# Query tiles 0 and 1 as a pair in the gates' ring, and projection steps spread over the attention's units

## The chip, the cores and the metric

The kernel runs on one core of a Trainium2 chip. The metric is the time of one execution on the device in microseconds, the median of several runs. Before the change it is 1763.04 us (three runs, 1761.94 to 1768.70).

## What is computed

One layer of a decoder trunk on 2048 rows of 1024 numbers in float32. A condition vector shifts and scales the rows; one wide product with `W_in` makes the queries, keys, values, the input of a pooling branch and four gates; sliding-window attention (16 query heads in 2 key/value groups, window 128, learned bias, one sink per head) and a causal pooling with four window widths run side by side; both are gated, projected, merged, projected again and normalised.

```python
u = x * (1.0 + scale[:, None, :]) + shift[:, None, :]
h = u @ w_in[l]
q, k, v, a_gate, p_in, p_gate, m_a, m_p = jnp.split(h, offsets, axis=-1)
a = sliding_window_sink_attention(q, k, v, sinks[l], bias, mask) * jax.nn.silu(a_gate)
a = a @ w_attn_proj[l]
p = jnp.einsum('bsgc,gcd->bsgd', multiscale_causal_pool(p_in), w_pool_mix[l]).reshape(B, S, POOL_WIDTH)
p = (p * pool_scale[l]) * jax.nn.silu(p_gate)
p = p @ w_pool_proj[l]
y = jax.nn.sigmoid(m_a) * a + jax.nn.sigmoid(m_p) * p
y = (y @ w_out[l]) * (1.0 + gate[:, None, :])
x = layer_norm(DEEPNORM_ALPHA * x + y, ln_gain[l], ln_bias[l])
```

## The kernel before

**Numbers and tiles.** Every float32 operand of a large product is split into a rounded part `hi` and a remainder `lo`, and each product is made of three matmuls, hi·hi, hi·lo and lo·hi (`mm3`, L138). One matmul takes a 128x128 weight block and 512 moving columns. The rows are worked on in two halves `s` = 0, 1 of 1024, each of two column tiles `t` (in the attention `st`) of 512. The output columns of `W_in` come in tiles `m` of 128: query tiles 0 to 7, one tile of keys, one of values, and eight each for the four gates.

**The ring.** A `Quad` (L276) is a pair of weight tiles. Its four output blocks (two weight tiles `mi` by two column tiles `t`) are made with seven block products in place of eight, in the manner of Strassen and Winograd: named by the moving set that each uses, B11, T1, T2, B21, T3, B22 and T4. Each block product is 4 x 3 = 12 matmuls (`product`, L336), so a pair costs 84 matmuls where the plain way costs 4 x 24 = 96. Its weights need sums of blocks (`sum1`, `mid`, `late`, on GpSimd) and three splits of 1024 columns and one of 512 (`pair_split`, `half_split`: hi on ScalarE, lo on VectorE). `ring` (L470) works through groups of two pairs, `front` opens a group (B11, T1), `back` finishes it, and `consume` takes each of the four blocks as it is ready, in the order (0,0), (1,1), (0,1), (1,0) of (`mi`, `t`). Other work hangs on counted positions (`hooks`, `steps`); in the second half the last group is finished pair by pair (`finish_pairs`, L433).

**Order of the halves.** For each half a ring makes keys, values and gates (17 pairs, nine groups, one of which has a single pair; in the first half the key/value pair is the first of the last group), the gates go to DRAM (`gates_d`), `first_q` (L735) makes query tile 0 the plain way, 48 matmuls for both column tiles, and then `attention` (L750) runs.

**The attention.** It has N = 64 units of one query block and two heads, numbered `n`; `j = n // 8` is the query tile that it uses. A unit's TensorE order is: scores of `n` (`score_mms`), transposes of the exponentials of unit n-2 (`turn_mms`), a piece of projection, values of unit n-2 (`value_mms`). Between the transposes and the values, ScalarE rounds the transposed block into `pth` and VectorE subtracts it into `ptl`. The projection pieces make the pooling tiles (`mix`, whose weights were folded with the pooling mix into `wmix_d`) and query tiles 1 to 7: 30 slots (tile, column tile) of 24 matmuls, two units to a slot, so every unit from 0 to 59 has 12 projection matmuls. Afterwards come the first products of the next ring (`fill_one`).

**What follows a slot.** `take_q` (L771) scales a finished query tile into the halves of `qs`: two ScalarE instructions, then two on VectorE. A pooling slot is followed by `pool_sums` (a ScalarE copy and up to four GpSimd additions), `pool_diff` (one on VectorE) and `finish` (GpSimd, then stores). A query tile's weights are loaded by `fetch`, rounded on ScalarE one unit later and subtracted on GpSimd another unit later. Engines work in program order: `pe`, `act`, `dve`, `pool` and `sp` are wrappers that keep it (L46); loads on `nc.sync` may be placed by the scheduler.

Of the kernel before, what the change touches and what calls it, by code (L numbers as in the profile page):

```python
# [19 lines left out]
P = 128  # L20
# [39 lines left out]
def kernel(  # L60
# [59 lines left out]
    ain_d = [set_store(f"ain{s}") for s in range(2)]  # L120
    pin_d = [set_store(f"pin{s}") for s in range(2)]
    gates_d = {n: dp.tile([2, KT, 2, P, CH], F32, name=f"{n}_d") for n in ("ag", "pg", "ma", "mp")}
    y_d = dp.tile([S // P, P, KT, P], F32, name="y_d")

    def cols(t, n):
# [606 lines left out]
    def moving_u():  # L732
        return (sets["B11"], sets["B21"]), (sets["T2"], sets["B22"])

    def first_q(ph, turn=None):  # L735

        raw, hi, lo = ph.spare(), ph.split(), ph.split()
        nc.sync.dma_start(raw, win[TQ])
        nc.scalar.copy(hi, raw)
        low(nc.vector, lo, raw, hi)  # L740
        accs = []
        for us in moving_u():
            acc, part = projection(us)
            part((hi, lo), 0, KT)
            if turn and not accs:
                turn(1)
            accs.append(acc)
        return accs

    def attention(ph, s, q0, nxt):  # L750
        tp = ph.t
        us = moving_u()
# [4 lines left out]
            nc.sync.dma_start(x, src)  # L757
            return x

        def fetch(kind, m):  # L760
            hi, lo = ph.split(), ph.split()
# [108 lines left out]
        slots = []  # L870
        for j in range(KT):
            slots += [("mix", j, 0), ("mix", j, 1)]
            if j + 1 < KT:
                slots += [("q", j + 1, 0), ("q", j + 1, 1)]
# [8 lines left out]
        tiles = {0: fetch(*slots[0][:2])}  # L883
# [36 lines left out]

        for n in range(N + 5):
            j, t, b = n // U, n // NB % 2, n % NB
            if n < N:
                lgs[n] = score_mms(j, n % U, b, qs[j, t])
            pt = None
# [67 lines left out]
            if pt is not None:  # L993
                pvs[n - 2] = value_mms((n - 2) // U, (n - 2) % U, k0, pth, ptl)


            w = n // 4 + 1
            if n % 4 == 0 and 2 * w < len(slots):
                tiles[w] = fetch(*slots[2 * w][:2])
            if w in tiles and tiles[w][0] is not None:  # L1000
                raw, hi, lo = tiles[w]
                if n % 4 == 1:
                    act.copy(by_two(hi), raw)
                if n % 4 == 2:
                    low(pool, by_two(lo), raw, by_two(hi))
            if n % U == 2 and j + 1 < KT:
                bts[j + 1] = bias_tile(j + 1)
            for st in range(2):
                if n % U == 6 + 2 * st - (U if st else 0) and (m := j + 1 - st) < KT and ("q", m, st) in accs:
                    qs[m, st] = take_q(accs.pop(("q", m, st)))  # L1010
            for what in puts:
                put(pool if n >= 64 else sp, *what)
            puts.clear()
# [10 lines left out]
            for st in range(2):  # L1024
                if n % U == 3 + 2 * st and (j, st) in sums:
                    pgs[j, st] = ld("pg", gates_d["pg"][s, j, st])
                if n % U == ((4, 6 + (j + 1 < KT))[st]) and (j, st) in sums:
                    pl = pool_diff(j, sums.pop((j, st)), accs.pop(("mix", j, st)))
                    finish("p", pin_d[s], j, st, pl, pgs.pop((j, st)))
            for st in range(2):  # L1030
                if n % U == 2 + 2 * st and ("mix", j, st) in accs:
                    sums[j, st] = pool_sums(j, st, accs["mix", j, st])
# [84 lines left out]
    def modulate(u, k):  # L1117
        dve.tensor_scalar(u, u, mod[:, 8 + k : 9 + k], mod[:, k : k + 1], ALU.mult, ALU.add)

    def gate_quads(s):  # L1120
        kv, turn = kv_quad(s)
        quads = [kv] if s else []
# [3 lines left out]
        last = quads[15:] if s else [kv, quads[15]]  # L1126
        return [quads[i : i + 2] for i in range(0, 14, 2)] + [quads[14:15], last], turn

    def gate_modulation(ph, m, cb):
        wa = []  # L1130
# [12 lines left out]
    def head(ph):  # L1143
# [90 lines left out]
            minus(xs[i][0], ts[i], xs[i][0])  # L1234
            minus(xs[4 + i][0], xs[4 + i][0], ts[i])

        groups, turn = gate_quads(0)
        grp = groups[0]
        opened = [[bank(), bank(), None, None] for q in grp]

# [71 lines left out]
        return groups, turn, opened, cb, rest  # L1312

    def first_phase(ph, groups, turn, opened, cb, rest):
# [28 lines left out]
        return ring(ph, groups, opened, hooks, [], lambda tick: first_q(ph, turn))  # L1343

    def second_phase(ph, opened, groups, turn):
        hooks = {(0, (8, 10)[i]): [lambda i=i: turn(i)] for i in range(2)}
        for p, name, half in ((0, "T3", 0), (1, "T3", 1), (3, "T4", 0), (5, "T4", 1)):
            hooks.setdefault((0, p), []).append(lambda name=name, half=half: fill_set(name, half, u1_d[name], sp))
        cb = ph.t.tile([P, D], F32, tag="cb", bufs=1, name="cb")

        def gate_rows():
            nc.scalar.dma_start(gate_d.rearrange("k p -> p k"), mod[:, 16:24], allow_slow_non_contiguous=True)
            nc.scalar.dma_start(cb, gate_d.rearrange("k p -> (k p)").partition_broadcast(P))

        hooks[(0, 2)] = [gate_rows]

        def load_wo(x, k):
            for n in range(2):
                sp.dma_start(cols(x, n), wout[k, n])

        halves_of = [(name, half) for name in set_names[:-1] for half in range(2)]
        for i in range(4):
            ks = (i, 4 + i)
            todo = sums_to(
                ph,
                wo_d,
                i,
                lambda x, r, ks=ks: load_wo(x, ks[r]),
                lambda x, r: dve.tensor_tensor(x, x, cb, ALU.mult),
                False,  # L1370
            )
# [6 lines left out]
        return ring(ph, groups, opened, hooks, [], lambda tick: first_q(ph), True)  # L1378

    def pairs(make):  # L1380
        return [[make(m), make(m + 2)] for m in (0, 4)]
# [130 lines left out]
```

## Time and profile before

| what | value |
|---|---|
| median of three runs | 1763.04 us |
| the profiled execution, its own time | 1766.1 us |
| its span, first to last instruction | 1763.9 us |
| VectorE, ScalarE, GpSimd busy in the span | 1206.9, 934.1, 794.2 us |
| first ring of gates, about | 52 to 401 us |
| first attention, about | 418 to 687 us |
| second ring, about | 696 to 1012 us |
| second attention, about | 1018 to 1285 us |
| output projections and norm | to 1764 us |

The stretches are read from the timeline of TensorE by the names of what its matmuls write and read: `lg<-kk,qs` are the attention's scores, `pt<-ident,L` its transposes, `pv<-pth,vv` and `pv<-ptl,vv` its values, `mm<-set,w_set` and `lg<-set,w_set` the products of the rings and of the projections. A duration of a matmul row spans its whole passage; matmuls overlap, so what one costs is the distance from start to start.

### The profile page before, as it was taken

The numbers are of one execution on the slowest core, as the hardware profiler recorded it, in microseconds if no ns is written. First come the engines' busy times: TensorE is split into PE (matmuls) and PEld (weight loads), VectorE is DVE, ScalarE is ACT, GpSimd is POOL, SyncE is SP. The second block draws the span as 40 slices with busy tenths as digits, with TensorE's granted clock in tenths as the row PEclk, the third lists the DMA queues.
The fourth block names the chain that finished last, engine by engine and source line by source line (L and its number), as shares of the span: only waits on it lengthen the run. The fifth ranks groups of instructions, "written<-read, shape, count | busy, mean of one in ns | idle before, by whom it ended". The sixth has DMA issues, their size and how long they took to land. (4 is left out here: it accounts for less than half of the span.)

```text
span 1763.9 us, 24990 instructions
## 1 busy us (share of the span) xinstructions
PE 1702.4 (97%) x8248; PEld 1427.4 (81%) x8248; DVE 1206.9 (68%) x2178; ACT 934.1 (53%) x1973; POOL 794.2 (45%) x618
## 2 busy tenths in 40 slices
PE   6899999999999998999999999999999989999997
PEld 5688888878888887888788888888888867888785
DVE  5977665655777776766655367777867676764777
ACT  4644444545777775544444377777734343423452
POOL 2154444431356567534434125456763562364542
PEclk9999999999999999999999999999999999999998
DMA  9385767844354567787777634544796675789442
GB/s 364 117 289 174 269 208 270 273 145 132 108 174 147 171 217 288 249 288 253 258 264 261 232 96 135 177 159 141 265 349 215 197 256 169 240 302 386 162 143 108
DMA packets 180466, 381.30 MB, mean 216 GB/s; under 512 B 18785, under 2 KB 39281, under 8 KB 180337
## 3 DMA queue, kind: packets, MB, share of 16 engines
q1 hardware_dynamic: 173696, 363.92, 60.5%
q0 software_dynamic: 3552, 11.56, 1.7%
q10 hardware_dynamic: 3088, 4.23, 0.8%
q8 instruction: 65, 1.06, 0.3%
q14 instruction: 65, 0.52, 0.1%
HBM read 244.35 MB, written 138.44 MB: 217 GB/s over the span
## 5 line engine op out<-in xcount | busy, mean ns | idle before, releaser
L56 PE MATMUL mm<-set_B,w_set 128*128 128x512 f32 x3240 | 798.7, 395 | 14.5 <-ACT u L376 6.3
L56 PEld LDWEIGHTS mm<-set_B,w_set 128*128 128x128 f32 x3240 | 603.3, 189 | 142.6 <-DVE w_set L132 10.3
L56 PE MATMUL lg<-set_T,w_set 128*128 128x512 f32 x2088 | 509.1, 394 | 18.4 <-DVE w_set L132 11.0
L56 PEld LDWEIGHTS lg<-set_T,w_set 128*128 128x128 f32 x2088 | 391.4, 189 | 111.0 <-DVE w_set L132 17.9
L132 DVE TENSOR_TENSOR w_set<-W,w_set 128x1024 fp32r<-128x1024 f32 x162 | 227.9, 1407 | 185.8 <-ACT w_set L325 180.8
L325 ACT CAST w_set<-W 128x1024 fp32r<-128x1024 f32 x162 | 169.8, 1049 | 251.6 <-PE mm L56 190.3
L56 PE MATMUL mm<-set_T,w_set 128*128 128x512 f32 x1080 | 265.5, 394 | 0.0
L56 PEld LDWEIGHTS mm<-set_T,w_set 128*128 128x128 f32 x1080 | 200.5, 188 | 41.0
L294 POOL TENSOR_TENSOR W<-W,A 128x512 f32<-128x512 f32 x56 | 82.1, 1466 | 227.6 <-DMA W<-in_win_dram 63.6
L303 POOL TENSOR_TENSOR W<-W 128x512 f32<-128x512 f32 x56 | 80.5, 1438 | 174.5 <-DVE w_set L132 165.2
L56 DVE TENSOR_TENSOR o<-pv,o 64x128 f32<-64x128 f32 x256 | 72.3, 283 | 89.8 <-ACT o L56 86.9
L56 ACT ACTIVATE L<-L,nm 128x257 f32<-128x257 f32 (+1 forms) x256 | 127.1, 498 | 9.3 <-DVE nm L56 3.9
L298 POOL TENSOR_TENSOR W<-W 128x512 f32<-128x512 f32 x56 | 90.5, 1618 | 84.7 <-DVE w_set L132 75.6
L56 DVE CUSTOM_DVE_ANT_0 L<-lg,bt,nsink 128x256 f32<-128x256 f32 (+1 forms) x256 | 111.6, 473 | 5.0 <-PE lg L56 0.8
L299 POOL TENSOR_TENSOR W<-W 128x512 f32<-128x512 f32 x56 | 84.7, 1513 | 37.9 <-DMA W<-in_win_dram 21.9
L56 POOL TENSOR_TENSOR w_set<-W,w_set 128x1024 fp32r<-128x1024 f32 x14 | 33.7, 2404 | 139.6 <-ACT w_set L56 96.9
L56 POOL TENSOR_TENSOR p<-nxt,pg 128x512 f32<-128x512 f32 x32 | 41.7, 1302 | 105.5 <-DVE sm L56 101.8
L56 ACT COPY o<-pv 64x256 f32<-64x256 f32 x128 | 47.3, 370 | 78.0 <-PE pv L56 77.2
L56 DVE TENSOR_TENSOR ptl<-pt,pth 128x512 fp32r<-128x512 f32 (+1 forms) x128 | 85.7, 669 | 1.9 <-ACT pth L56 1.7
L56 PE MATMUL lg<-kk,qs 128*128 128x256 f32 (+1 forms) x512 | 80.5, 279 | 0.0
L56 ACT ACTIVATE L<-L,sm 128x256 f32<-128x256 f32 (+1 forms) x128 | 64.2, 502 | 29.8 <-DVE sm L56 29.8
L56 ACT CAST pth<-pt 128x512 fp32r<-128x512 f32 (+1 forms) x128 | 73.5, 574 | 10.3
(212 smaller groups left out, 2296.3 us busy)
## 6 DMA issues: line engine op xcount, KB each, us to landing
W<-in_win_dram SPq DMA_DIRECT2D x48, 512.0 KB, 5.5
w_set<-wmix_d SPq DMA_DIRECT2D x32, 512.0 KB, 5.4
W<-in_win_dram SPq DMA_DIRECT2D x34, 256.0 KB, 3.7
A<-in_win_dram SPq DMA_DIRECT2D x34, 256.0 KB, 5.1
ag_d<-sig SPq DMA_DIRECT2D x32, 256.0 KB, 3.8
pg_d<-sig SPq DMA_DIRECT2D x32, 256.0 KB, 4.0
ma_d<-sig SPq DMA_DIRECT2D x32, 256.0 KB, 4.0
mp_d<-sig SPq DMA_DIRECT2D x32, 256.0 KB, 4.0
```

What stands on the lines that cost most here:

```text
L56: return lambda *args, **kw: self.tc.keep_in_program_order(op(*args, **kw))
L132: engine.tensor_tensor(dst, src, as32(hi), ALU.subtract)
L294: e.tensor_tensor(self.w[:, 1, :], self.w[:, 2, :], self.a22, ALU.add)
L298: e.tensor_tensor(x[:, 1, :], x[:, 1, :], x[:, 0, :], ALU.subtract)
L299: e.tensor_tensor(x[:, 2, :], x[:, 0, :], x[:, 2, :], ALU.subtract)
L303: e.tensor_tensor(x[:, 3, :], x[:, 3, :], x[:, 1, :], ALU.subtract)
L325: a.copy(by_two(hi), raw)
```

## The change

Three things are altered.

1. `first_q` goes. Query tiles 0 and 1 become the 18th pair of the ring (`q_quad`), in the last group of each half. The two blocks of tile 0 stay in PSUM and are handed to the attention; the two of tile 1 are stored to DRAM (`q_d`), straight from the ring's tile for one and through a ScalarE copy for the other.
2. In the attention, tile 1 is loaded back from `q_d` two units ahead and taken by `take_q` in units 6 and 8. The slots for query tile 1 go: 28 slots remain, in the order mix 0, mix 1, q 2, mix 2, q 3, ... q 7, mix 7.
3. The 28 x 8 = 224 projection steps (three matmuls each) are spread by `upto` over units 0 to 59: unit 0 has 7 steps, now ahead of its scores, each later one 3 or 4. What follows a slot is timed by `done`, the unit in which the slot ends: `take_q` one unit later, `pool_sums` one, the gate's load two, `pool_diff` three or four. The weights of the first slot (mix 0) go into a buffer `W` of the ring in place of two of the split weights' buffers.

```diff
+    q_d = [dp.tile([2, 2, P, CH], F32, name=f"q{s}_d") for s in range(2)]
...
-    def first_q(ph, turn=None):
-
-        raw, hi, lo = ph.spare(), ph.split(), ph.split()
-        nc.sync.dma_start(raw, win[TQ])
-        nc.scalar.copy(hi, raw)
-        low(nc.vector, lo, raw, hi)
...
-            part((hi, lo), 0, KT)
...
+        order = (("mix", 0), ("mix", 1), ("q", 2), ("mix", 2), ("q", 3), ("mix", 3), ("q", 4), ("mix", 4), ("q", 5), ("mix", 5), ("q", 6), ("mix", 6), ("q", 7), ("mix", 7))
+        slots = [(kind, m, st) for kind, m in order for st in range(2)]
...
+        def upto(n):
+            return (0 if n == 0 else min(n + 1, 61)) * KT * len(slots) // 61
+
+        def unit_of(k):
+            return next(n for n in range(60) if upto(n + 1) > k)
+
+        first = [unit_of(KT * i) for i in range(len(slots))]
+        done = {x: unit_of(KT * i + KT - 1) for i, x in enumerate(slots)}
+
+        def project(n):
+            k = upto(n)
+            while k < upto(n + 1):
+                i = k // KT
+                end = min(KT * (i + 1), upto(n + 1))
+                if k == KT * i:
+                    accs[slots[i]], parts[i] = projection(us[slots[i][2]])
+                parts[i](tiles[i // 2][1:], k - KT * i, end - KT * i)
+                k = end
+
+        room = ph.weights().rearrange("p a c -> p (a c)").bitcast(F32R)
+        tiles = {0: fetch(*order[0], [cols2(room, n) for n in range(2)])}
...
+            if n == 0:
+                project(n)
...
-            i = n // 2
-            if i < len(slots):
-                kind, m, st = slots[i]
-                if n % 2 == 0:
-                    accs[kind, m, st], parts[i] = projection(us[st])
-                parts[i](tiles[i // 2][1:], 4 * (n % 2), 4 * (n % 2) + 4)
+            if 0 < n < 60:
+                project(n)
...
+            for w in range(1, len(order)):
+                at = first[2 * w - 2]
+                if n == at:
+                    tiles[w] = fetch(*order[w])
+                if n in (at + 1, at + 2) and tiles[w][0] is not None:
+                    raw, hi, lo = tiles[w]
+                    if n == at + 1:
+                        act.copy(by_two(hi), raw)
+                    else:
+                        low(pool, by_two(lo), raw, by_two(hi))
...
+            for m in range(1, 2):
+                for st in range(2):
+                    at = 8 * m - 2 + 2 * st
+                    if n == at - 2:
+                        raw_q[m, st] = ld("raw_q", q_d[s][m, st])
+                    if n == at:
+                        qs[m, st] = take_q(raw_q.pop((m, st)))
+            for x in [x for x in done if x[0] == "q" and n == done[x] + 1]:
+                qs[x[1:]] = take_q(accs.pop(x))
...
+                if n == at + 3 + (st == 1 and m + 1 < KT):
+                    pl = pool_diff(m, sums.pop((m, st)), accs.pop(x))
...
+    def q_quad(s, m, first):
+
+
+        def consume(ph, mi, t, src):
+            k = m + mi
+            if k == 0:
+                first[t] = src
+                return
+            x = src
+            if (mi, t) != (1, 1):
+                x = ph.c("qk")
+                nc.scalar.copy(x, src)
+            defer(2, lambda: sp.dma_start(q_d[s][k, t], x))
+
+        return Quad((win[TQ + m], win[TQ + m + 1]), consume)
...
+        quads += [q_quad(s, m, q0) for m in (0,)]
+        if s == 0:
+            quads.insert(-1, kv)
+        return [quads[i : i + 2] for i in range(0, len(quads), 2)], turn, q0
```

More of the change, by code (lines that the diff above doesn't have):

```diff
@@ L733, in moving_u @@
         return (sets["B11"], sets["B21"]), (sets["T2"], sets["B22"])
-    def first_q(ph, turn=None):
-        raw, hi, lo = ph.spare(), ph.split(), ph.split()
-        nc.sync.dma_start(raw, win[TQ])
-        nc.scalar.copy(hi, raw)
-        low(nc.vector, lo, raw, hi)
-        accs = []
-        for us in moving_u():
-            acc, part = projection(us)
-            part((hi, lo), 0, KT)
[L745 to L748, printed above, removed]
     def attention(ph, s, q0, nxt):
@@ L758, in ld, with fetch @@
             return x
-        def fetch(kind, m):
-            hi, lo = ph.split(), ph.split()
+        def fetch(kind, m, lent=None):
+            hi, lo = lent or (ph.split(), ph.split())
             if kind == "mix":
@@ L879, in stage @@
             return tp.tile([P, CH], F32, tag=f"{kind}{half}{t}", bufs=1, name=f"{kind}{half}{t}")
+        def upto(n):
[15 more added lines that the diff above has]
+        tiles = {0: fetch(*order[0], [cols2(room, n) for n in range(2)])}
         qs = {(0, t): take_q(q0[t]) for t in range(2)}
         bts = {0: bias_tile(0)}
-        tiles = {0: fetch(*slots[0][:2])}
+        raw_q = {}
         parts, accs, sums = {}, {}, {}
@@ L994, in attention @@
                 pvs[n - 2] = value_mms((n - 2) // U, (n - 2) % U, k0, pth, ptl)
[L997 to L1005, printed above, removed]
+            for w in range(1, len(order)):
[8 more added lines that the diff above has]
+                        low(pool, by_two(lo), raw, by_two(hi))
             if n % U == 2 and j + 1 < KT:
                 bts[j + 1] = bias_tile(j + 1)
-            for st in range(2):
-                if n % U == 6 + 2 * st - (U if st else 0) and (m := j + 1 - st) < KT and ("q", m, st) in accs:
-                    qs[m, st] = take_q(accs.pop(("q", m, st)))
+            for m in range(1, 2):
[7 more added lines that the diff above has]
+                qs[x[1:]] = take_q(accs.pop(x))
             for what in puts:
@@ L1023, in attention @@
                 act.copy(opened[0][4], opened[0][0])
[L1024 to L1032, printed above, removed]
+            for x, at in done.items():
+                kind, m, st = x
+                if kind == "q":
+                    continue
+                if n == at + 2:
+                    pgs[m, st] = ld("pg", gates_d["pg"][s, m, st])
+                if n == at + 3 + (st == 1 and m + 1 < KT):
+                    pl = pool_diff(m, sums.pop((m, st)), accs.pop(x))
+                    finish("p", pin_d[s], m, st, pl, pgs.pop((m, st)))
+            for x, at in done.items():
+                if x[0] == "mix" and n == at + 1:
+                    sums[x[1:]] = pool_sums(*x[1:], accs[x])
             for x in [x for x in outs if n == x[0] * U + x[1] * NB + NB + 2]:
@@ L1235, in rest_sums @@
             minus(xs[4 + i][0], xs[4 + i][0], ts[i])
-        groups, turn = gate_quads(0)
+        groups, turn, q0 = gate_quads(0)
         grp = groups[0]
@@ L1311, in head, with first_phase @@
         ]
-        return groups, turn, opened, cb, rest
-    def first_phase(ph, groups, turn, opened, cb, rest):
+        return groups, turn, q0, opened, cb, rest
+    def first_phase(ph, groups, turn, q0, opened, cb, rest):
         hooks = {}
@@ L1342, in first_phase, with second_phase @@
             at(-1, 3 + half, lambda half=half: build(ph, "T2", half, b12_d))
-        return ring(ph, groups, opened, hooks, [], lambda tick: first_q(ph, turn))
-    def second_phase(ph, opened, groups, turn):
+        ring(ph, groups, opened, hooks, [], lambda tick: turn(1))
+        return q0
+    def second_phase(ph, opened, groups, turn, q0):
         hooks = {(0, (8, 10)[i]): [lambda i=i: turn(i)] for i in range(2)}
@@ L1377, in second_phase @@
             hooks.setdefault((-1, 3 + half), []).append(lambda half=half: fill_set("T2", half, u1_d["B12"]))
-        return ring(ph, groups, opened, hooks, [], lambda tick: first_q(ph), True)
+        ring(ph, groups, opened, hooks, [], None, True)
+        return q0
     def pairs(make):
```

8 lines of the change are left out of this document (1 added, 7 removed).

## The prediction

> **What bounds the kernel now.** I read the page's head and the engines' busy time, then stretches of the span, then the chain of waits for the price of a matmul, then the timeline unit by unit.
>
> ```profile
> span 1763.9 us, 24990 instructions
> PE 1702.4 (97%) x8248; PEld 1427.4 (81%) x8248; DVE 1206.9 (68%) x2178; ACT 934.1 (53%) x1973; POOL 794.2 (45%) x618
> ```
>
> ```profile
> 200.00:380.00 180.00, 177.70 (x831) 147.30 (x830) 106.68 (x106) 78.34 (x119) 83.47 (x63) 1.00 0.71 245
> 430.00:500.00 70.00, 70.00 (x403) 61.42 (x402) 51.81 (x166) 52.28 (x161) 29.79 (x25) 1.00 0.40 125
> 600.00:700.00 100.00, 93.44 (x514) 80.30 (x513) 76.19 (x206) 68.47 (x192) 70.85 (x60) 0.97 0.69 245
> 860.00:1000.00 140.00, 138.37 (x610) 113.92 (x609) 78.45 (x78) 64.18 (x100) 53.05 (x36) 1.00 0.73 258
> 1000.00:1200.00 200.00, 200.00 (x1126) 174.51 (x1125) 133.14 (x422) 143.07 (x418) 81.87 (x63) 1.00 0.47 146
> ```
>
> The columns after the stretch's length are the busy times of TensorE, its weight loads, VectorE, ScalarE and GpSimd, the granted clock, the DMA share and GB/s. In the rings TensorE is busy but for 1 or 2%; in both attentions it never rests. So removed matmuls count in full, as long as nothing takes their place as the thing waited for. The price of one:
>
> ```profile
> 1470.77 2.72 PE mm L56 x12
> 1478.93 10.88 PE mm L56 x48
> ```
>
> 2.72 / 12 = 0.227 us (the 0.39 us of the groups' rows is passage, not pitch).
>
> A full TensorE says nothing of how near its inputs come to being late. That is read from three neighbouring units of the second attention, 8, 9 and 10, whose values end at 1053, 1057 and 1061 us:
>
> ```profile
> 1050.28 3.02 PE L56 MATMUL mm<-set_B,w_set 128*128 128x512 f32 x12
> 1053.25 0.29 PE L56 MATMUL pv<-ptl,vv 128*128 128x256 f32 x1
> 1054.45 3.02 PE L56 MATMUL mm<-set_B,w_set 128*128 128x512 f32 x12
> 1057.43 0.29 PE L56 MATMUL pv<-ptl,vv 128*128 128x256 f32 x1
> 1058.63 3.00 PE L56 MATMUL mm<-set_T,w_set 128*128 128x512 f32 x12
> 1061.58 0.29 PE L56 MATMUL pv<-ptl,vv 128*128 128x256 f32 x1
> ...
> 1051.48 0.69 DVE L56 TENSOR_TENSOR ptl<-pt,pth 128x512 fp32r<-128x512 f32 x1
> 1053.49 1.39 DVE L56 SCALAR_TENSOR_TENSOR qs<-mm,qs 64x512 fp32r<-64x512 f32 x2 [0.86 <-ACT qs L56]
> 1054.89 0.17 DVE L56 RECIPROCAL sm<-sm 128x2 f32<-128x2 f32 x1
> 1056.51 0.68 DVE L56 TENSOR_TENSOR ptl<-pt,pth 128x512 fp32r<-128x512 f32 x1
> 1060.29 0.68 DVE L56 TENSOR_TENSOR ptl<-pt,pth 128x512 fp32r<-128x512 f32 x1
> ...
> 1052.27 1.18 ACT L56 ACTIVATE qs<-mm 64x512 fp32r<-64x512 f32 x2
> 1055.15 0.51 ACT L56 ACTIVATE L<-L,sm 128x256 f32<-128x256 f32 x1 [0.95 <-DVE sm L56]
> 1055.68 0.59 ACT L56 CAST pth<-pt 128x512 fp32r<-128x512 f32 x1
> 1057.40 1.03 ACT L56 CAST w_set<-W 128x1024 fp32r<-128x1024 f32 x1
> ```
>
> The values need `ptl`; the slack is from the end of `ptl` to the start of `pv<-ptl`. Unit 8, with nothing extra before it: 1051.48 + 0.69 = 1052.17 to 1053.25, **1.08 us**. Unit 9, behind a `take_q`: 1057.19 to 1057.43, **0.24 us**. The take holds ScalarE and then, in series, VectorE; the reciprocal comes only at 1054.89, the scaling, `pth` and `ptl` are queued behind it, and TensorE waits for `ptl`. Unit 10, behind the rounding of a query tile's weights (1057.40): 1060.97 to 1061.58, **0.61 us**. With 12 projection matmuls as cover, none of these is late.
>
> **The change part by part.**
>
> *Matmuls.* Per half the ring's pair costs 84 and `first_q`'s 48 go: +36. The attention loses two slots: -48. Net -12, in both halves -24: 24 x 0.227 = **-5.4 us**.
>
> *The ring's other work.* The pair adds two more splits of 1024, one of 512, four GpSimd sums, two evictions. All lie under 84 matmuls (19 us) in stretches where VectorE is busy 78 of 140 us, ScalarE 64 and GpSimd 53; a split costs 1.4 + 1.05 us by the rows below. Nothing for that, and 1 or 2 us if the cover failed. The odd single pair becomes a full group; the ring's late part already shows no wait there.
>
> ```profile
> L132 DVE TENSOR_TENSOR w_set<-W,w_set 128x1024 fp32r<-128x1024 f32 x162 | 227.9, 1407 | 185.8 <-ACT w_set L325 180.8
> L325 ACT CAST w_set<-W 128x1024 fp32r<-128x1024 f32 x162 | 169.8, 1049 | 251.6 <-PE mm L56 190.3
> ```
>
> *DMAs.* The two query tiles' weights are loaded in another shape with the same bytes; each half adds two stores and two loads of 256 KB. On SP's queue the first bias tiles now stand behind the store of `qk`, where they stood behind the last store of a gate; both follow the last product's eviction.
>
> *The attention's opening.* Before, from the end of the last T4 (400.76 + 5.75 less its tail, 406.3) to the first score are 48 matmuls and a transpose; now 21 matmuls. What must fit under them:
>
> ```profile
> 400.76 5.75 PE L56 MATMUL lg<-set_T,w_set 128*128 128x512 f32 x24
> 417.75 0.56 PE L56 MATMUL lg<-kk,qs 128*128 128x128 f32 x4
> 424.62 0.38 PE L56 MATMUL pt<-ident,L 128*128 128x128 f32 x2
> ...
> 407.55 1.03 SPq L56 DMA_DIRECT2D bt<-e_rep  x2
> ...
> 420.60 0.35 DVE L56 CUSTOM_DVE_ANT_0 L<-lg,bt,nsink 128x128 f32<-128x128 f32 x1
> 422.85 0.28 DVE L56 TENSOR_SCALAR L<-L,sm 128x128 f32<-128x128 f32 x1
> ...
> bt<-e_rep SPq DMA_DIRECT2D x2, 256.0 KB, 4.9
> ```
>
> Counted from the end of T4: the value turn and 21 matmuls end near 5.2 us. The four takes need 4 x 0.6 on ScalarE and 4 x 0.7 on VectorE, near 5.1. The bias tile is issued at 1.3 and lands 4.9 later, 6.2. From the first VectorE step to the scaled block are 423.13 - 420.60 = 2.5 us: 8.7. The first transposes stand behind two scores and 12 more matmuls, near 9.3. It fits by half a microsecond: 0, at most 3 us a half if the bias tile comes late.
>
> *The spread.* 224 steps over 61 don't come out even. Unit 0 has 21 matmuls; of units 1 to 59, 40 have 12 and 19 have 9 (units 2, 5, 8 and so on to 56). A unit with 9 covers 3 x 0.227 = 0.68 us less. The plain slack of 1.08 bears it. The slack of 0.24 behind a take doesn't: 0.44 us of wait, whether the short unit is the one behind the take or the one that holds it, since the take starts when ScalarE is through with its own unit's exponentials, which hang on the scores, not on the projection. `done` puts the takes in units 6, 8, 10, 13, 19, 21, 28, 30, 37, 39, 45, 47, 54 and 56. By the short units next to them:
>
> - 10, 19, 28, 47, 56: 0.44 each, 2.20.
> - 8 and 37 hold a `pool_diff` too, on VectorE between the take and the reciprocal; before, takes and these never met. It takes 0.60 (666.33 to 666.93 below): 1.04 each, 2.08.
> - 13, 30 and 39 also hold a rounding of query weights, ahead of the take on ScalarE; these too never met before. It holds ScalarE 1.0 us. Beside a short unit (13): 1.44. Beside full ones (30, 39): 1.0 - 0.24 = 0.76 each. Together 2.96.
> - A rounding alone before a short unit (4, 22): 0.61 - 0.68, 0.07 each, 0.14.
> - 6, 21, 45, 54: nothing.
>
> ```profile
> 666.33 0.67 DVE L56 SCALAR_TENSOR_TENSOR nxt<-nxt,mm 128x512 f32<-128x512 f32 x1
> 666.93 0.15 DVE L56 RECIPROCAL sm<-sm 128x2 f32<-128x2 f32 x1
> ```
>
> Sum 7.4 us a half, **+14.8 us** in both. A wait of TensorE in a stage where it had none is time; nothing later gives it back, since every later unit has its own 12 or 9. Bounds: counted without the meetings, 8 x 0.44 x 2 = 7.0 us; with half as much again for waits that push the next unit, 22.
>
> *Tile 1 read back.* The trace has no such load; the nearest are the gates' loads in the same buffers:
>
> ```profile
> DMA to landing us min/median/max: 2.6/3.5/8.9
> ```
>
> The second one waits for the take in unit 6 to free its buffer (about 2.4 us into unit 7) and is wanted near the end of unit 8, some 5 us later. At the median 3.5 it is there; at 8.9 ScalarE stands 4 us, and behind it on ScalarE stand all exponentials. I take 0.3 a half, +0.6; bounds 0 and 8.
>
> *Sum.* 1766.1 (the profiled execution) - 5.4 + 14.8 + 0.6 = 1776.1, which is +10.0. The profiled execution is 3 us above the median of the runs, so for the median 1763.0 + 10.0 = **1773 us**.
>
> **The rivals.**
>
> 1. *Only the matmuls count.* The short cover is never found out, because takes run early enough beside it. Then -5.4: 1757.6, faster than before. For it: TensorE is the only engine above 75%. Against it: 0.24 us behind every take, read above, and 0.68 removed. It decides if a short unit behind a take shows a slack above zero. Chance 0.10.
> 2. *The waits are there, the meetings are free.* Rounding, `pool_diff` and take hide in each other's idle time; 7.0 - 5.4 = +1.6: 1764.6. For it: VectorE idles 0.86 us before the take's part. Against it: that idle is the take's own ScalarE half, which a rounding ahead of it lengthens. Chance 0.15.
> 3. *Late loads.* The bias tile or tile 1 comes late in both halves: 1773 + 8 = 1781. For it: SP's queue is served in order and landings reach 8.9. Against it: the median fits. Chance 0.10.
> 4. *The clock falls.* Frequent small rests bring TensorE's granted clock down. The one rest of 6.29 us (below) stands in the stretch with 0.97; at 0.97 over both attentions (some 265 us each) it would be 3% of 530, 16 us: 1789. Against it: 0.5 to 1.4 us is far from 6.29, and the clock is 1.00 everywhere else. Chance 0.03.
>
> ```profile
> 695.76 1.65 PE L56 MATMUL mm<-set_B,w_set 128*128 128x512 f32 x3 [6.29 <-ACT u L376]
> ```
>
> The Trainium skill (TensorE: Matmul & The Clock Gate, "A second HAM failure mode: psum-queue depth-cycling") says that micro-idling between groups of matmuls can make the clock gate swing; by that rule the fourth case would be the likely one. This trace agrees only that one long rest goes with a lower clock; no row shows short ones doing it.
>
> **How the numbers follow.** The forecast has 0.62, its own range 1767 to 1779; the rivals 0.10, 0.15, 0.10, 0.03. The range for 8 in 10 leaves out the first and the fourth and reaches from the second to the third: 1764 to 1781. Half a per cent, about what a measurement of this kernel can tell from no change, is 8.8 us: slower means above 1771.9. The forecast lies just above; about two thirds of its 0.62 and the cases 3 and 4 are slower by more, 0.56; a third of it and cases 1 and 2 are within, 0.41; faster by as much would need more than all matmuls saved, 0.03.
>
> **What would show it.** In the profile after: the list of what TensorE waited for, empty now in the attentions, has `pv <- DVE ptl` some ten times a half, 0.4 to 1.5 us each, together about 15 us, the longest behind units 8, 13 and 37; TensorE's busy share in the attentions falls from 100% to about 97%; 24 matmuls fewer by count; the opening without a wait above 1 us; the rest of 6.3 us between first attention and second ring still there. Wrong would be: no waits for `ptl`, waits for `raw_q` or `bt`, or a rest in the rings near the last group.

## The result, and the profile after

The changed kernel takes 1771.83 us (median of 10 runs, 1769.43 to 1775.40) where the kernel before takes 1761.93 us beside it (median of 10, 1757.82 to 1768.70). The ratio is 1.0055, with a 95% interval of 1.0042 to 1.0068: 9.9 us slower, 7.4 to 12.0. The forecast was +10.0.

The page's head for the kernel after:

```profile
span 1769.9 us, 24992 instructions
...
PE 1701.8 (96%) x8224; PEld 1422.5 (80%) x8224; DVE 1212.4 (68%) x2188; ACT 941.5 (53%) x1983; POOL 803.5 (45%) x624
```

TensorE has 8248 - 8224 = 24 instructions fewer, as counted, and yet the span is longer. The stretches of the two attentions say where (columns as in the prediction: length, busy TensorE, weight loads, VectorE, ScalarE, GpSimd, then granted clock, DMA share and GB/s):

```profile
430.00:500.00 70.00, 68.15 (x386) 58.41 (x386) 50.83 (x170) 55.09 (x169) 30.60 (x27) 1.00 0.41 139
500.00:600.00 100.00, 97.60 (x558) 83.89 (x557) 75.45 (x241) 75.81 (x230) 54.95 (x46) 1.00 0.43 149
1000.00:1200.00 200.00, 195.58 (x1084) 167.71 (x1083) 137.48 (x414) 141.09 (x406) 81.53 (x63) 1.00 0.48 164
```

Before, TensorE's 70.00 of 70 and 200.00 of 200 were full; now it is busy for 97.4 to 97.8%. The granted clock is 1.00 as before. What TensorE waited for, in the first attention (426 to 690 us) and then in the second (1026 to 1300 us); the columns are us in total, times, longest:

```profile
PE pv L56 <- DVE ptl L56: 3.7, 9, 0.6
PE pv L56 <- ACT pth L56: 0.7, 2, 0.5
...
PE pv L56 <- DVE ptl L56: 4.3, 10, 0.5
PE pv L56 <- ACT pth L56: 0.7, 2, 0.5
```

In the kernel before the same list is empty for the first attention. The values wait for `ptl`, and twice a half for `pth` already. How such a wait is read, at unit 14, which stands behind the take and the rounding in unit 13, in the timeline after:

```profile
478.92 0.28 PE L56 MATMUL pv<-pth,vv 128*128 128x256 f32 x1
479.04 0.29 PE L56 MATMUL pv<-ptl,vv 128*128 128x256 f32 x1
...
479.41 0.63 PE L56 MATMUL lg<-kk,qs 128*128 128x256 f32 x4
...
481.02 1.55 PE L56 MATMUL mm<-set_T,w_set 128*128 128x512 f32 x6
483.08 0.38 PE L56 MATMUL pv<-pth,vv 128*128 128x256 f32 x1 [0.51 <-ACT pth L56]
484.02 0.38 PE L56 MATMUL pv<-ptl,vv 128*128 128x256 f32 x1 [0.55 <-DVE ptl L56]
...
478.08 1.03 ACT L56 CAST w_set<-W 128x1024 fp32r<-128x1024 f32 x1
479.02 1.20 ACT L56 ACTIVATE qs<-mm 64x512 fp32r<-64x512 f32 x2
481.91 0.51 ACT L56 ACTIVATE L<-L,sm 128x256 f32<-128x256 f32 x1 [1.30 <-DVE sm L56]
482.45 0.59 ACT L56 CAST pth<-pt 128x512 fp32r<-128x512 f32 x1
...
480.25 1.39 DVE L56 SCALAR_TENSOR_TENSOR qs<-mm,qs 64x512 fp32r<-64x512 f32 x2 [2.01 <-ACT qs L56]
481.65 0.17 DVE L56 RECIPROCAL sm<-sm 128x2 f32<-128x2 f32 x1
483.28 0.68 DVE L56 TENSOR_TENSOR ptl<-pt,pth 128x512 fp32r<-128x512 f32 x1
```

It is the chain that the prediction read before the change: rounding (478.08) and take (479.02) on ScalarE, the take on VectorE (480.25), only then the reciprocal (481.65), `pth` (482.45) and `ptl`, which ends at 483.96; the values start at 484.02. In a unit without a wait the lo value follows the hi value by 0.12 us (478.92 to 479.04). Here it follows by 0.94, so this wait is 0.82 us. The bracket lists 0.55 because the modelled end of the matmul before it hangs over into the rest. The wait for `pth` is read from starts too: from a unit's first score to its first hi value is 2.99 us in a short unit without a wait (492.74 to 495.73 in unit 17) and 3.67 here (479.41 to 483.08), so it is 0.68 us, where the bracket lists 0.51. Measured by starts in this way, the waits stand behind these units, beside what was forecast for them:

| extra work in the unit ahead | forecast, each | first attention | second attention |
|---|---|---|---|
| take by a short unit: 10, 19, 28, 47, 56 | 0.44 | 0.81, 0.62, 0.54, 0.40, 0.36 | 0.64, 0.54, 0.54, 0.54, 0.53 |
| take and `pool_diff`: 8, 37 | 1.04 | 0.28, 0.68 and 0.34 for `pth` | 0.46, 0.68 and 0.34 for `pth` |
| take, rounding and short unit: 13 | 1.44 | 0.82, and 0.68 for `pth` | 0.81, and 0.68 for `pth` |
| take and rounding: 30, 39 | 0.76 | 0.81, 0.60 | 0.80, 0.81 |
| rounding alone: 4, 22 | 0.07 | 0, 0.23 | 0, 0.23 |

The waits for `pth` stand behind units 37 (listed as 0.17 and 0.18) and 13. The waits for `ptl` sum to 6.15 and 6.58 us; no other unit shows one above 0.1. Those for `pth` sum to 2.2 us in both attentions, with one of 0.16 behind unit 10 that the list leaves out. By the stage as a whole: from the attention's first matmul to its last value the kernel before takes 268.7 and 272.0 us. Without 48 matmuls at 0.227 that would be 257.8 and 261.1; the kernel after takes 265.7 and 269.6, so 7.9 and 8.5 us are lost, 16.4 in both.

One thing came back in the first ring. First the timeline of TensorE before, in the group that has a single pair, then the same passage after:

```profile
366.55 0.73 PE L56 MATMUL mm<-set_B,w_set 128*128 128x512 f32 x2 [0.84 <-ACT w_set L325]
367.91 2.55 PE L56 MATMUL mm<-set_B,w_set 128*128 128x512 f32 x10 [0.62 <-DVE w_set L132]
```

```profile
364.37 2.88 PE L56 MATMUL mm<-set_B,w_set 128*128 128x512 f32 x12
367.09 2.93 PE L56 MATMUL lg<-set_T,w_set 128*128 128x512 f32 x12
369.86 2.93 PE L56 MATMUL mm<-set_B,w_set 128*128 128x512 f32 x12
```

There a pair alone doesn't give its splits enough matmuls to hide under; with the query pair in its group they do. All three profiles with the old group list these two waits, 1.5 to 1.7 us together, and none of the seven with the new one does. The rest between first attention and second ring is 4.67 us here, where it was 6.29; six experiments with the same ring have 4.64 to 6.51, so that difference can't be put down to the change:

```profile
696.27 8.96 PE L56 MATMUL mm<-set_B,w_set 128*128 128x512 f32 x26 [4.67 <-ACT u L377]
```

### The profile page after: what moved, and what is told of

It reads as the page before. It is cut to its first block, busy times and chain, and to the rows that moved or that the text cites. A ratio compares the mean times of both kernels' runs of the same rounds, so it can differ in the third digit from the quotient of the medians.

```text
span 1769.9 us, 24992 instructions
## 1 busy us (share of the span) xinstructions
PE 1701.8 (96%) x8224; PEld 1422.5 (80%) x8224; DVE 1212.4 (68%) x2188; ACT 941.5 (53%) x1983; POOL 803.5 (45%) x624
## 5 line engine op out<-in xcount | busy, mean ns | idle before, releaser
L56 PE MATMUL mm<-set_B,w_set 128*128 128x512 f32 x3096 | 768.5, 395 | 12.4 <-DVE w_set L133 5.5
L56 PEld LDWEIGHTS mm<-set_B,w_set 128*128 128x128 f32 x3096 | 577.3, 189 | 134.2 <-DVE w_set L133 10.6
L56 PE MATMUL lg<-set_T,w_set 128*128 128x512 f32 x2160 | 523.6, 392 | 17.3 <-DVE w_set L133 9.3
L56 PEld LDWEIGHTS lg<-set_T,w_set 128*128 128x128 f32 x2160 | 404.2, 188 | 110.8 <-DVE w_set L133 14.9
L326 ACT CAST w_set<-W 128x1024 fp32r<-128x1024 f32 x168 | 176.3, 1050 | 266.8 <-PE mm L56 204.9
L56 PE MATMUL mm<-set_T,w_set 128*128 128x512 f32 x1032 | 257.6, 394 | 0.0
L56 PEld LDWEIGHTS mm<-set_T,w_set 128*128 128x128 f32 x1032 | 192.3, 189 | 39.5
L304 POOL TENSOR_TENSOR W<-W 128x512 f32<-128x512 f32 x58 | 81.8, 1410 | 189.0 <-DVE w_set L133 178.7
L299 POOL TENSOR_TENSOR W<-W 128x512 f32<-128x512 f32 x58 | 92.0, 1587 | 89.5 <-DVE w_set L133 80.4
L300 POOL TENSOR_TENSOR W<-W 128x512 f32<-128x512 f32 x58 | 94.6, 1630 | 43.8 <-DMA W<-in_win_dram 27.6
L56 POOL TENSOR_TENSOR nxt<-vb 128x512 f32<-128x512 f32 (+3 forms) x32 | 34.2, 1068 | 122.7 <-ACT vb L56 122.7
L56 DVE TENSOR_TENSOR k_lo<-spare,k_hi 128x512 fp32r<-128x512 f32 x61 | 61.4, 1009 | 30.0 <-ACT k_hi L56 13.2
```

The source lines that it names most:

```text
L56: return lambda *args, **kw: self.tc.keep_in_program_order(op(*args, **kw))
L299: e.tensor_tensor(x[:, 1, :], x[:, 1, :], x[:, 0, :], ALU.subtract)
L300: e.tensor_tensor(x[:, 2, :], x[:, 0, :], x[:, 2, :], ALU.subtract)
L304: e.tensor_tensor(x[:, 3, :], x[:, 3, :], x[:, 1, :], ALU.subtract)
L326: a.copy(by_two(hi), raw)
```

## The experiments

All ratios are to the kernel before, run on the same chip. Its median there was 1761.93 us for the change itself, 1766.36 (23 runs) for the four experiments below it and 1765.98 (17 runs) for the other three and the last profile.

| experiment | ratio and interval | waits for `ptl` by starts, us, first and second attention |
|---|---|---|
| the change itself | 1.0055 [1.0042, 1.0068] | 6.15, 6.58 |
| short units placed by hand | 1.0011 [0.9997, 1.0024] | 2.34, 0.78 |
| short units padded | 1.0137 [1.0120, 1.0153] | 2.85, 2.73 |
| roundings moved off the takes | 1.0023 [1.0012, 1.0033] | 4.75, 5.03 |
| takes in two parts | 1.0045 [1.0032, 1.0058] | 3.22, 4.13 |
| the spread alone | 1.0053 [1.0034, 1.0071] | 4.01, 4.48 |
| the pair alone, two units a slot | 1.0098 [1.0082, 1.0114] | 5.49, 3.53 |
| placed, and `pool_diff` one unit later | 0.9976 [0.9963, 0.9989] | 1.40, 1.58 |

Listed waits for `pth` come on top, above all 2.6 us in the kernel placed by hand and 5.3 in the pair alone with two units a slot. A difference between two ratios carries both intervals, some 3 us together. The attentions by the stage tell differences more sharply: from first matmul to last value both together take 540.7 us before and 535.3 after the change, and 526.1, 550.7, 531.3 and 531.1 in the first four experiments.

**Short units placed by hand.** The same 19 short units, in other places: away from takes and roundings. Since `done` follows, so do the meetings.

```diff
+        short = (2, 3, 5, 23, 24, 25, 26, 32, 33, 34, 35, 41, 42, 43, 44, 50, 51, 52, 53)
...
-            return (0 if n == 0 else min(n + 1, 61)) * KT * len(slots) // 61
+            return 4 * n + 3 * (n > 0) - sum(x < n for x in short)
```

> The changed kernel with the same 19 units of 9 projection matmuls a half, but at other units: 2, 3, 5, 23-26, 32-35, 41-44, 50-53, so that almost none is the unit of a take or the one behind it, and no rounding of weights falls into a take's unit. Matmuls and everything else as after the change. Theory (a short unit costs only beside a take or where extras meet): TensorE's waits for ptl and pth fall from about 14 us in both halves to about 4; some 10 us faster than the changed kernel, level with the kernel before, 1760 to 1764 us. Rival (the number of short units counts, wherever they stand, or the loss lies in the ring or the opening): 1772 as the changed kernel.

Measured 1.0011 and 1768.15 us, above the 1760 to 1764 expected, though 7.8 us less than the change by the ratios and 9.2 by the attentions. The same matmuls and the same loads, and most of the loss is gone, only because 19 units, and what is timed by them, lie elsewhere: the cause is where the cover is short and what it meets there, not how much work there is. What was left showed something that I had not counted, in units 43 and 52. Timelines of VectorE, TensorE and GpSimd in this kernel, in unit 52 of the second attention, and behind the last dots TensorE and VectorE in the same unit of the first:

```profile
1235.15 0.69 DVE L56 SCALAR_TENSOR_TENSOR nxt<-nxt,mm 128x512 f32<-128x512 f32 x1 [1.19 <-POOL nxt L56]
...
1237.12 0.38 PE L56 MATMUL pv<-pth,vv 128*128 128x256 f32 x1 [0.30 <-ACT pth L56]
1237.97 0.38 PE L56 MATMUL pv<-ptl,vv 128*128 128x256 f32 x1 [0.47 <-DVE ptl L56]
...
1232.52 1.29 POOL L300 TENSOR_TENSOR W<-W 128x512 f32<-128x512 f32 x1
1233.77 1.35 POOL L56 TENSOR_TENSOR nxt<-nxt 128x512 f32<-128x512 f32 x1
...
635.19 0.39 PE L56 MATMUL pv<-pth,vv 128*128 128x256 f32 x1 [1.63 <-ACT pth L56]
633.22 0.69 DVE L56 SCALAR_TENSOR_TENSOR nxt<-nxt,mm 128x512 f32<-128x512 f32 x1 [2.74 <-POOL nxt L56]
```

`pool_diff` on VectorE stands 1.19 us for the last of GpSimd's window sums, because a weight sum of the next ring (1232.52) went between them. In the first attention it stands 2.74 us there and TensorE 1.63. A due time counted in units is a shorter time when the units are shorter.

**Short units padded.** Three products with a block of zeros are added in every unit that has 9, so each unit covers 12; the sums stay as they are. It adds 57 matmuls a half, 57 x 0.227 = 12.9 us.

```diff
+        zero = tp.tile([P, P], F32R, tag="zero", bufs=1, name="zero")
...
+                short = upto(n + 1) - upto(n) == 3 and k == upto(n)
+                if short and k > KT * i:
+                    pad(i)
...
+                mm(accs[slots[i]], zero, us[slots[i][2]][0][:, 0, 0, :], start=False, stop=False)
```

> The changed kernel with three matmuls by a block of zeros added to each of the 19 short units of a half, so that every unit from 1 to 59 has 12: 114 matmuls more, 114 x 0.227 = 25.9 us of TensorE. Theory (the cover is what is missing): the waits behind takes alone go, those where a rounding or a pool_diff meets a take stay in part, from 14 to about 6 us: 25.9 - 8 = 18 us slower than the changed kernel, about 1790 us. Rival (the waits don't hang on the cover): 26 us slower, 1798 us.

Measured 1.0137 and 1791.03 us. Against the changed kernel that is (1.0137 - 1.0055) x 1766 = 14.5 us, and by the attentions 15.4, for 25.9 us of added matmuls: some 10 to 11 us of them fill rests. What TensorE still waited for:

```profile
PE pv L56 <- DVE ptl L56: 3.4, 8, 0.5
```

By starts, the waits left are those behind units 13, 30, 37 and 39 (0.33 to 0.81 us each) and 0.29 once behind 10. With full cover the plain takes (10, 19, 28, 47, 56) are nearly free, and the meetings with a rounding, and one of the two with `pool_diff`, are not. The prediction's split into the two kinds is shown, with one exception, the meeting with `pool_diff` in unit 8.

**Roundings moved off the takes.** Where the rounding of a gate's or query tile's weights would fall into a take's unit, it comes one unit later.

```diff
+        taken = {at + 1 for x, at in done.items() if x[0] == "q"}
...
+                at += at + 1 in taken
```

> The changed kernel with the rounding of a query tile's weights (and the subtraction behind it) one unit later where it shared a unit with a take: from 13, 30, 39 to 14, 31, 40. Theory (a meeting costs ScalarE's 1.0 us on top): the waits in unit 14 fall by about 1.0, those in 31 and 40 of 0.8 each go or shrink to 0.1; 2.4 us a half, 4 to 5 us faster than the changed kernel, about 1767 us. Rival (meetings are free): 1772 us, waits in units 31 and 40 unchanged.

Measured 1.0023, so (1.0055 - 1.0023) x 1766 = 5.7 us less than the change, and 4.0 by the attentions. The waits of 0.60 to 0.81 behind 30 and 39 go (in the second attention 0.16 and 0.20 us stand behind 31 and 40, where the rounding now is; in the first 0.29 behind 43, which has a `pool_diff`), the one behind 13 falls from 0.82 to 0.53 and its wait for `pth` goes, and those of the plain takes stay.

**Takes in two parts.** Each take is cut into its two 64-row parts, done in neighbouring units, where the scores leave time for it.

```diff
...
-            for x in [x for x in done if x[0] == "q" and n == done[x] + 1]:
-                qs[x[1:]] = take_q(accs.pop(x))
+            for x in [x for x in done if x[0] == "q"]:
+                two = done[x] + 2 < 8 * x[1] + 4 * x[2] - 1
+                if n == done[x] + 1:
+                    qs[x[1:]] = take_q(accs[x], (0,) if two else (0, 1))
+                if two and n == done[x] + 2:
+                    take_q(accs[x], (1,), qs[x[1:]])
```

> The changed kernel with each take_q made in two parts in two neighbouring units (one head's ScalarE and VectorE instruction each) where the scores don't need it at once. The same instructions. Theory (a take costs because ScalarE's two instructions and VectorE's two stand in series ahead of the reciprocal): the waits fall from 14 to about 4 us in both halves, left in units 14, 23, 31 and 41; about 10 us faster than the changed kernel, 1760 to 1764 us. Rival (the sum of work on ScalarE and VectorE in a short unit decides): 1772 us, twice as many, smaller waits.

A miss: 1.0045, only 1.8 us below the change, where 10 were expected. The attentions are 4.2 us shorter, but the stretch between them is 340.1 us long, 2.6 more than with the change, though the edit doesn't touch it. The waits for `ptl` fall by 2.93 and 2.45 us, but new ones stand behind both units of a split take, and in each half one of 1.1 us for `L`, which no kernel had before. VectorE, GpSimd and TensorE there:

```profile
551.80 2.34 DVE L56 TENSOR_SCALAR L<-L,sm 128x256 f32<-128x256 f32 x1
...
551.63 2.37 POOL L56 TENSOR_TENSOR w_set<-W,w_set 128x1024 fp32r<-128x1024 f32 x1
...
554.20 0.55 PE L56 MATMUL pt<-ident,L 128*128 128x128 f32 x3 [1.11 <-DVE L L56]
```

VectorE's scaling of one head's block, 0.34 us elsewhere (422.85 in the prediction's rows, for half the columns 0.28), lasts 2.34: it ends 0.14 us after GpSimd's instruction does (551.63 + 2.37 = 554.00). So a shorter piece of work doesn't help if it brings another piece into GpSimd's way.

**The spread alone.** The kernel before, with only the third part of the change: `first_q` and the 30 slots stay, no matmul goes, the 240 steps are spread by the same formula and `done` times what follows.

```diff
+        def upto(n):
+            return (0 if n == 0 else min(n + 1, 61)) * KT * len(slots) // 61
...
-                if n % U == 6 + 2 * st - (U if st else 0) and (m := j + 1 - st) < KT and ("q", m, st) in accs:
-                    qs[m, st] = take_q(accs.pop(("q", m, st)))
+            for x in [x for x in done if x[0] == "q" and n == done[x] + 1]:
+                qs[x[1:]] = take_q(accs.pop(x))
```

> The kernel before (query tile 0 made by first_q, tile 1 in the attention, 30 slots) with the spread and its timing by done alone: unit 0 has 21 projection matmuls, units 14, 29 and 44 have 9, all others 12; no matmul fewer. The roundings of query weights now fall into the takes' units 8, 16, 24, 32 and 40. Theory (a meeting of rounding and take costs 0.76 beside a full unit, a short unit beside a take 0.44): waits for ptl in units 9, 17, 25, 33, 41 of 0.8 each and in 15 of 0.4, about 4 us a half, 8 us in all: 8 us slower than the kernel before, ratio 1.004 to 1.006. Rival (only the shorter cover costs): three short units a half, less than 1 us, ratio 1.000.

Measured 1.0053 (6.0 to 12.5 us). Only three units are short here, so most of the 8.5 us of waits are meetings of takes with roundings, which the old grid of 4 and 8 units had kept apart. The spread alone is enough to make the kernel slower.

**The pair alone, two units a slot.** The pair in the ring and the 28 slots as in the change, but in the old grid: units 0 to 55 have 12 projection matmuls, 56 to 59 none.

```diff
-            return (0 if n == 0 else min(n + 1, 61)) * KT * len(slots) // 61
+            return min(4 * n, KT * len(slots))
```

> The changed kernel's pair in the ring and its 28 slots, but each slot over two whole units as before the change: units 0 to 55 have 12 projection matmuls, 56 to 59 none. Theory (a unit's wait is what its cover falls short of the slack): no waits up to 55 but one of 0.4 in unit 9, where pool_diff meets a take; in 56 to 59 1.08 - 2.84 = 1.8 each, 7 us a half; in all 14 to 15 us less 5.4 of matmuls, about 9 us slower than the kernel before, as the changed kernel. Rival (waits come from the ring's pair or the read-back, not from the cover): waits as in the changed kernel, in units 9, 11, 14, 20 and so on.

A miss of another kind: 1.0098, 17 us slower where about 9 were expected. The place was right, the size not. TensorE's timeline at the four empty units, and then the stretches around them with their granted clock (after the five busy times):

```profile
650.43 0.28 PE L56 MATMUL pv<-pth,vv 128*128 128x256 f32 x1
...
654.59 0.28 PE L56 MATMUL pv<-pth,vv 128*128 128x256 f32 x1
...
658.04 0.64 PE L56 MATMUL lg<-kk,qs 128*128 128x256 f32 x4
658.52 0.60 PE L56 MATMUL pt<-ident,L 128*128 128x128 f32 x4
659.86 0.39 PE L56 MATMUL pv<-pth,vv 128*128 128x256 f32 x1 [0.74 <-ACT pth L56]
661.10 0.38 PE L56 MATMUL pv<-ptl,vv 128*128 128x256 f32 x1 [0.84 <-DVE ptl L56]
...
664.87 1.06 PE L56 MATMUL lg<-kk,qs 128*128 128x256 f32 x4
665.72 1.06 PE L56 MATMUL pt<-ident,L 128*128 128x128 f32 x4
...
674.35 0.28 PE L56 MATMUL pv<-pth,vv 128*128 128x256 f32 x1
```

```profile
650.00:655.00 5.00, 5.00 (x31) 4.43 (x30) 2.44 (x9) 2.98 (x11) 4.43 (x4) 1.00 0.00 0
655.00:660.00 5.00, 3.16 (x23) 2.49 (x22) 3.75 (x15) 4.43 (x15) 3.12 (x5) 1.00 0.38 126
660.00:665.00 5.00, 2.93 (x13) 2.04 (x14) 4.41 (x16) 4.38 (x13) 4.15 (x4) 0.70 1.01 374
665.00:670.00 5.00, 3.79 (x16) 3.10 (x15) 3.89 (x12) 3.04 (x10) 3.87 (x4) 0.50 1.03 417
670.00:675.00 5.00, 5.00 (x25) 4.41 (x24) 3.50 (x9) 3.12 (x8) 4.92 (x4) 0.78 0.74 288
```

Without cover every unit is paced by ScalarE and VectorE, with a rest ahead of `pth` and another ahead of `ptl`. After some 7 us in which TensorE is busy for 60% (655 to 662, where 0.70 over the third stretch puts the fall), its granted clock falls to 0.50, and the same four score matmuls take 0.85 us from start to start (664.87 to 665.72) where they took 0.48. The passage from 654.59 to 674.35 is 19.76 us. Four empty units at 4.16 - 2.72 = 1.44 and one full one at 4.16 would be 9.9 (4.16 us is the distance of the values, 650.43 to 654.59, of neighbouring full units), so 9.8 us are lost; in the second half the same passage loses 10.4. With the 5.4 saved that makes +14.8, and 2.0 us of small waits in the first half bring it to +16.8. These, 0.3 us each in units 11, 19, 27 and so on to 51 and once in 53, were not expected, and why only the first half has them is not shown.

**Placed, and `pool_diff` one unit later.** The first experiment's idea, with what it taught: short units in other places again, and `pool_diff` of both column tiles four units after the slot.

```diff
+        short = (2, 3, 5, 15, 16, 17, 18, 23, 24, 25, 27, 32, 33, 34, 36, 42, 43, 45, 47)
...
-                if n == at + 3 + (st == 1 and m + 1 < KT):
+                if n == at + 3 + (m + 1 < KT):
```

> The changed kernel with its 19 short units at 2, 3, 5, 15 to 18, 23 to 25, 27, 32 to 34, 36, 42, 43, 45, 47, away from takes and from the late units where GpSimd has the long pooling sums, and pool_diff of the first column tile one unit later (four behind its slot), so that VectorE doesn't wait for GpSimd. Theory: waits in the attentions fall to 2 to 4 us in both halves; the 24 matmuls saved come through: 1 to 4 us faster than the kernel before, ratio 0.998 to 0.9995, and 2 to 4 us faster than with the first placing. Rival (what is left in the first placing, ratio 1.001, is the pair's own cost in the ring or the read-back): ratio 1.001 again.

Measured 0.9976, 1760.84 us (median of 12): faster than the kernel before, a little more than the 1 to 4 us expected, and 0.9976 / 1.0055 = 0.992 of the changed one. What the new places and what the later `pool_diff` give isn't told apart. All that the attention's list of waits still shows, in the first half, is

```profile
PE pv L56 <- DVE ptl L56: 0.4, 1, 0.4
```

**The kernel before, once more.** A second profiled execution, to see what differs without any edit.

> The kernel before once more, for a second profile: how far the waits in the rings and at the passage from the first attention to the second ring (6.3 us in the first profile) differ between two executions of one program. By each theory 1762 to 1767 us and no wait of TensorE in the attentions.

It took 1771.83 us, and its span is 1770.0, 6.1 us longer than the first profile's 1763.9. The attentions agree: 269.0 and 272.0 us, against 268.7 and 272.0, though the first has one listed wait for `ptl` here, of 0.23 us. The first attention starts 4.7 us later, 422.43 in place of 417.75. The time of one profiled execution is thus not good to better than some 6 us, and the difference of the two spans, +6.0 from before to after, says little; stages that agree between executions, and medians, do.

## Why the prediction was right

*Matmuls, -5.4.* Right: 24 fewer by count, and where nearly no waits are left (the last version) the kernel is faster than before, by 4.2 us (1.9 to 6.5); -5.4 and its 3.0 us of waits make -2.4, which lies within.

*The spread, +14.8.* Right in kind, place and size: 14.9 us by starts (12.7 for `ptl`, 2.2 for `pth`), 16.4 by the stages. All ten units that were named with more than 0.07 us show a wait, and 6, 21, 45 and 54, which were not, show none. The padded kernel shows the two kinds apart. The size by kind was less exact: a plain take by a short unit costs 0.36 to 0.81 where I wrote 0.44. Of the meetings with `pool_diff` the one in 37 came as worked out, 0.68 + 0.34 = 1.02 against 1.04. The one in 8, which was forecast among the longest, cost only 0.28 and 0.46. Its take is that of tile 1, which needs no product of the attention; that this makes it cheaper is not shown. The meetings with roundings came as worked out: 0.60 to 0.81 against 0.76, and 1.50 at unit 13 against 1.44.

*The ring, 0.* Wrong by a little. "The ring's late part already shows no wait there" was read from a stretch that is 98.7% busy; its timeline has 0.84 + 0.62 us in the single pair's group, and they went. From the last value of the first attention to the first matmul of the second takes 331.6 us before, in both profiles; 36 matmuls more would make 339.8, and the change has 337.5. Six experiments with the same ring have 336.8 to 340.3, so 1 us a half, give or take two, is what can be said, and that of the second ring alone: the start of the first attention differs by 4.7 us between the two profiles of the kernel before.

*The opening, 0, and tile 1, +0.6.* The opening shows no wait: the scores start at 427.75, the first transposes at 431.88, neither behind an idle time. No wait for `raw_q` or `bt` is in any list, so tile 1 costs 0.

*Sum.* With 16.4 for the spread and about -2 for the rings: -5.4 + 16.4 - 2 = +9. The +10.0 hit nearer than its terms did, since two errors of 1 to 2 us cancel; that is luck.

*The rivals.* Only the matmuls count: excluded by the waits. The meetings are free: excluded by the padded kernel, where they are nearly all that stays, though it held in part for the one in unit 8. Late loads: no such wait. The clock falls: not in the attentions of this kernel, 1.00 with 23 listed rests of at most 0.6 us (0.82 by starts), those of different units at least 8 us apart; but the mechanism exists, and the pair alone shows what it takes. The Trainium skill (TensorE: Matmul & The Clock Gate, "A second HAM failure mode: psum-queue depth-cycling") says of another kernel that frequent micro-idling between groups of matmuls makes the gate swing. The empty units agree with that (0.50 after about 7 us at 60% busy), the attention at 97.5% doesn't show it.

## What to carry to other kernels

A full engine hides how near each of its inputs is to being late: take the distance from the producer's end to the consumer's start, unit by unit, before moving cover about. When work is spread evenly, everything that was timed by the old grid meets anew; place the short units by hand where nothing extra stands, and count due times in microseconds, not in units. And a stage without cover should be kept shorter than the time after which the clock falls, or be given other work.

## What was not expected of the hardware

VectorE's `L<-L,sm` waits for GpSimd, its neighbour `ptl` does not. The forms of VectorE's instructions in the first attention of the changed kernel (busy us, mean ns, then idle before):

```profile
L56 DVE TENSOR_TENSOR ptl<-pt,pth 128x512 fp32r<-128x512 f32 x56 | 38.4, 686 | 0.8 <-ACT pth L56 0.7
...
L56 DVE TENSOR_SCALAR L<-L,sm 128x256 f32<-128x256 f32 x56 | 31.5, 563 | 0.0
```

Taken one by one against GpSimd's timeline in both attentions, 58 of 120 such scalings start while GpSimd does nothing, and they take 0.34 to 0.35 us. Of the 62 that start inside a GpSimd instruction, 41 end 0.14 to 0.16 us after the end of one, however long they waited for it, up to 1.45 us here and 2.34 in the kernel with split takes; 16 others run beside grouped rows, whose inner ends the view doesn't show, and five that start at most 0.15 us before GpSimd's end take 0.34. The Trainium skill (SBUF — State Buffer, "Who interferes with whom") says that a `tensor_scalar` can run in a mode that takes the pair of ports which VectorE shares with GpSimd, and that whichever of the two issues first holds the pair for its whole instruction while the other is blocked. The 41 rows agree. On a path with 0.24 us of slack it matters which GpSimd instruction runs beside it.

The second finding is the clock: half speed after about 7 us at 60% busy, in the kernel with empty units above. The rest of 4.67 us between attention and ring, which began at 691.6, does the same in the changed kernel:

```profile
690.00:696.00 6.00, 1.60 (x8) 0.98 (x6) 3.98 (x8) 2.87 (x6) 4.64 (x4) 0.95 1.02 420
696.00:701.00 5.00, 4.73 (x11) 3.77 (x12) 1.88 (x3) 0.81 (x2) 2.54 (x5) 0.50 1.02 401
701.00:706.00 5.00, 5.00 (x21) 4.04 (x21) 2.48 (x3) 3.51 (x4) 1.28 (x1) 0.88 0.56 195
```

A mean of 0.95 over the first 6 us is half speed from about 695.4, some 4 us into the rest; 0.50 holds through the next stretch, and 0.88 over the last is half speed until about 702.2, 6 us after work resumed at 696.27. Both figures take the clock to be either 1.00 or 0.50, the only values that it holds for long in these views. By an estimate, half speed for those 6 us costs some 3 us beside the rest itself.
